# A layer normalisation without weights: a fourth early row, one wait taken out of a loop, and two reciprocals moved from VectorE to GpSimd

## The chip, the cores and the metric

One core of one Trainium2 chip. The metric is device time in microseconds (us). Before the change the median of three runs was 318.32 us (318.27 to 318.82). Times of instructions and packets are from the start of the profiled span, which is some 1.8 us shorter than the measured time of the same run. In the profile's lines DVE is VectorE, POOL is GpSimd, ACT is ScalarE and SP is SyncE; ACTq and SPq issue their DMAs.

## The reference

```python
# x: 32 x 512 x 1024, float32; eps = 1e-5
mean = np.mean(x, axis=-1, keepdims=True)
var = np.var(x, axis=-1, keepdims=True)
return ((x - mean) / np.sqrt(var + eps)).astype(np.float32)
```

16384 rows of 1024 numbers: 64 MiB are read and 64 MiB are written, once each.

## The kernel before

A tile is 8 rows for each of the 128 partitions (4 MiB); the last two tiles have 6 and 2 rows. The ring holds 48 rows, six tiles. SyncE issues the loads; ScalarE issues three rows of tile 3 ahead of everything and later all stores. For each tile VectorE takes statistics, GpSimd combines them, ScalarE takes the root, VectorE the reciprocal, GpSimd forms nmr = -mean x rstd, ScalarE normalises in place and issues the store.

```python
TILES = (8,) * 15 + (6, 2)
SLOT, SLOTS = 8, 6
FIRST, TURNS = 3, 2
HALVES = (4, 4)          # tile 0 goes in two halves
EARLY, AHEAD = 3, 3      # tile 3: three rows ahead, on ScalarE's queue
# ...
    for k in range(AHEAD):
        load(nc.scalar, EARLY, k, 1, ahead)
    # ... for each tile t, on SyncE, once the stores of the ring's rows are done:
        first = AHEAD if t == EARLY else 0
        dma = load(nc.sync, t, first, K - first, landed[t])
# ...
    def vector(t, arrived, turn):
        K, row, at = plan[t]
        if t == EARLY:
            nc.vector.wait_ge(ahead, 16 * AHEAD)
        statistics(at, K, landed[t], arrived)
        nc.vector.reciprocal(
            out=rstd[:, at : at + K], in_=std[:, at : at + K]
        )._wait_ge(rooted[t], turn).then_inc(inverse, 1)

    nc.vector.memset(eps_t[:], eps_val)
    nc.vector.memset(power[:], -1.0)
    # ... tiles 0 to 2, then tiles 3 to 14 in a loop of two turns, then tiles 15 and 16
# ... GpSimd, after the sums of a group:
        if t:
            n = inverse, t
        else:                               # tile 0: GpSimd's own power of -1
            n = gp(g.tensor_tensor(out=rstd[:, at : at + K], in0=std[:, at : at + K],
                                   in1=power[:, :K], op=ALU.pow), rooted[t], i + 1)
        ready.append(gp(g.tensor_mul(out=nmr[:, at : at + K], in0=nm,
                                     in1=rstd[:, at : at + K]), *n))
# ... ScalarE, at the end of a tile:
            nc.scalar.dma_start(
                out=rows_of(o2, row, K), in_=ring[:, at : at + K, :]
            )._wait_ge(act, row + K).then_inc(stored[t], 16)
# ... GpSimd, last of all: waits for the stores
    for t in range(len(plan)):
        if t in owner.values():
            nc.gpsimd.wait_ge(stored[t], sixteens(stored, t))
```

Of the kernel before, what the change touches and what calls it, by code (L numbers as in the profile page):

```python
# [13 lines left out]
FIRST, TURNS = 3, 2  # L14


HALVES = (4, 4)


EARLY, AHEAD = 3, 3  # L20


@with_exitstack
def kernel(
# [6 lines left out]
    nc = tc.nc  # L31
# [19 lines left out]
    plan, row = [], 0  # L51
# [40 lines left out]
    for t, (K, row, at) in enumerate(plan):  # L92
        for n in HALVES if t == 0 else (K,):
            groups.append((t, at, n))
# [3 lines left out]
    second, ahead = nc.alloc_semaphore("second_half"), nc.alloc_semaphore("ahead")  # L98

    def load(engine, t, first, n, sem):  # L100
        K, row, at = plan[t]
        return engine.dma_start(
            out=ring[:, at + first : at + first + n, :],
            in_=rows_of(x2, row, K)[:, first : first + n, :],
        ).then_inc(sem, 16)
# [4 lines left out]
    for t, (K, row, at) in enumerate(plan):  # L110
# [4 lines left out]
        if t == 0:  # L115
            load(nc.sync, t, 0, HALVES[0], landed[t])
            load(nc.sync, t, HALVES[0], HALVES[1], second)
            continue
# [6 lines left out]
    def statistics(at, n, sem, value):  # L125
        for k in range(at, at + n):
            for s in range(NSUB):
                i = nc.vector.bn_stats(  # L128
                    out=stats[:, k, s, :],
                    in_=ring[:, k, s * BN_MAX : (s + 1) * BN_MAX],  # L130
                )
                if k == at and s == 0:
                    i._wait_ge(sem, value)
        i.then_inc(taken, 1)

    def vector(t, arrived, turn):
        K, row, at = plan[t]
        if t == EARLY:
            nc.vector.wait_ge(ahead, 16 * AHEAD)
        statistics(at, K, landed[t], arrived)  # L140
        nc.vector.reciprocal(  # L141
            out=rstd[:, at : at + K], in_=std[:, at : at + K]
        )._wait_ge(rooted[t], turn).then_inc(inverse, 1)

    nc.vector.memset(eps_t[:], eps_val)  # L145
    nc.vector.memset(power[:], -1.0)  # L146
    statistics(0, HALVES[0], landed[0], 16)
    statistics(HALVES[0], HALVES[1], second, 16)
    for t in range(1, FIRST):
        vector(t, 16, 1)  # L150
    turn = nc.vector.alloc_register("turn")
    nc.vector.reg_mov(turn, 1)
    nc.vector.addr_align(128, max_nops=0)
    with nc.vector.Fori(16, 16 * TURNS + 1, 16) as arrived:
        for t in range(FIRST, FIRST + SLOTS):
            vector(t, nc.vector.lower_val(arrived), turn)
        nc.vector.reg_add(turn, turn, 1)
    for t in range(FIRST + TURNS * SLOTS, len(plan)):
        vector(t, 16, 1)
# [4 lines left out]
    def gp(i, sem, value):  # L164
        nonlocal npool
        i._wait_ge(sem, value).then_inc(pool, 1)
        npool += 1
        return pool, npool

    g = nc.gpsimd  # L170
    for i, (t, at, K) in enumerate(groups):
        parts = stats[:, at : at + K].rearrange("p g s (h c) -> p g (s h) c", h=2)
        mean4, m2 = parts[:, :, :, 1], parts[:, :, :, 2]
        nm, d, h = nmean[:, at : at + K], dev[:, :K], half[:, :K]
        n = gp(
            g.tensor_tensor(out=h, in0=mean4[:, :, 0:2], in1=mean4[:, :, 2:4], op=ALU.add),  # L176
            taken,
            i + 1,
        )
        n = gp(g.tensor_tensor(out=nm, in0=h[:, :, 0], in1=h[:, :, 1], op=ALU.add), *n)  # L180
        n = gp(
            g.tensor_scalar(out=nm, in0=nm, scalar1=-1.0 / H, scalar2=None, op0=ALU.mult),  # L182
            *n,
        )
        n = gp(
            g.tensor_tensor(  # L186
                out=d, in0=mean4, in1=nm.unsqueeze(2).to_broadcast([P, K, H]), op=ALU.add
            ),
            *n,
        )  # L190
        n = gp(g.tensor_mul(out=d, in0=d, in1=d), *n)  # L191
        n = gp(
            g.tensor_scalar(  # L193
                out=d, in0=d, scalar1=float(D // H), scalar2=None, op0=ALU.mult
            ),
            *n,
        )
        n = gp(g.tensor_tensor(out=d, in0=d, in1=m2, op=ALU.add), *n)  # L198
        n = gp(g.tensor_tensor(out=h, in0=d[:, :, 0:2], in1=d[:, :, 2:4], op=ALU.add), *n)  # L199
        summed.append(  # L200
            gp(
                g.tensor_tensor(  # L202
                    out=ss[:, at : at + K], in0=h[:, :, 0], in1=h[:, :, 1], op=ALU.add
                ),
                *n,
            )
        )
        if t:
            n = inverse, t
        else:  # L210
            n = gp(
                g.tensor_tensor(  # L212
                    out=rstd[:, at : at + K],
                    in0=std[:, at : at + K],
                    in1=power[:, :K],
                    op=ALU.pow,
                ),
                rooted[t],
                i + 1,
            )  # L220
        ready.append(
            gp(
                g.tensor_mul(  # L223
                    out=nmr[:, at : at + K], in0=nm, in1=rstd[:, at : at + K]
                ),
                *n,
            )
        )
# [65 lines left out]
```

## Time and profile before

| | before |
|---|---|
| median time | 318.32 us |
| span of the profiled run (318.44 us) | 316.66 us |
| first data packet starts | 1.93 us |
| last data packet ends | 314.43 us |
| last store's landing seen by its semaphore | 314.90 us |
| from that landing to the end of the span ("wind-up" below) | 1.75 us |

These are the page's first line and the last line of its part on DMA issues (queue, count, KB each, us from issue to landing):

```profile
span 316.7 us, 712 instructions
...
out_dram<-ring ACTq DMA_DIRECT2D x1, 1024.0 KB, 9.2
```

The lines that carry the bound stand in the prediction.

### The profile page before, as it was taken

To read this page: it belongs to the slowest core of one execution; us is meant where nothing else is said; L and a number is where in the kernel's file an instruction comes from. 1 tells how busy PE (TensorE), PEld (TensorE's weight loads), DVE (VectorE), ACT (ScalarE), POOL (GpSimd) and SP (SyncE) were. 2 spreads that over 40 slices of the span, in tenths; PEclk is the share of its full clock that TensorE was granted. 3 is DMA by queue.
4 is the path that set the end of the run, shared out by engine and by line. 5 is a ranking of instruction groups with operands and counts; after the bars stand their busy time and mean duration, and the time that the engine had idled before them with its cause. 6 is when DMAs were issued, how large, how long until landed. Compare 5 with 4: busy or idle time off the path is not lost.

```text
span 316.7 us, 712 instructions
## 1 busy us (share of the span) xinstructions
DVE 157.0 (50%) x274; ACT 153.3 (48%) x147; POOL 43.6 (14%) x186
## 2 busy tenths in 40 slices
DVE  0656584916529074380934709256191652918300
ACT  1065094947091561907429083380924709156740
POOL 0151202020200202001020110202002020021300
DMA  7999999999999999999999999999999999999996
GB/s 288 440 447 414 397 430 430 445 418 447 426 439 423 439 435 430 439 430 435 426 435 430 447 414 447 426 439 435 435 426 435 426 435 435 444 412 429 449 419 261
DMA packets 5476, 134.25 MB, mean 424 GB/s; under 512 B 608, under 2 KB 608, under 8 KB 992
## 3 DMA queue, kind: packets, MB, share of 16 engines
q10 hardware_dynamic: 2880, 68.68, 50.4%
q1 hardware_dynamic: 2592, 65.54, 48.5%
q14 instruction: 4, 0.03, 0.0%
HBM read 67.11 MB, written 67.11 MB: 424 GB/s over the span
## 4 chain that ended last, share of the span: by engine, by line
DVE 43%; another core or an unknown queue 23%; DMA 12%; POOL 10%; ACT 4%; issue 4%; SPq 0%; ACTq 0%; DVEq 0%
DVE stats L128 42%; DMA ring<-in_x_dram 12%; ACT ring L240 3%; ACT std L232 1%; POOL dev L193 1%; POOL dev L198 1%; POOL dev L186 1%; POOL nmean L182 1%; POOL dev L191 1%; POOL half L176 1%; POOL half L199 1%; POOL nmean L180 1%; POOL ss L202 1%; DVE rstd L141 1%
## 5 line engine op out<-in xcount | busy, mean ns | idle before, releaser
L128 DVE BATCH_NORM_STATS2 stats<-ring 128x6 f32<-128x512 f32 x256 | 153.7, 678 | 92.7 <-DMA ring<-in_x_dram 92.7
L240 ACT ACTIVATE ring<-ring,nmr,rstd 128x1024 f32<-128x1024 f32 x128 | 146.8, 1226 | 11.7 <-POOL nmr L223 11.7
L232 ACT ACTIVATE std<-ss,eps_t 128x8 f32<-128x8 f32 (+3 forms) x18 | 5.4, 299 | 138.4 <-POOL ss L202 138.0
L176 POOL TENSOR_TENSOR half<-stats 128x16 f32<-128x16 f32 (+3 forms) x18 | 4.1, 230 | 235.4 <-DVE stats L128 235.4
L141 DVE RECIPROCAL rstd<-std 128x8 f32<-128x8 f32 (+2 forms) x16 | 3.2, 200 | 52.3 <-ACT std L232 52.3
L193 POOL TENSOR_SCALAR dev<-dev 128x32 f32<-128x32 f32 (+3 forms) x18 | 5.1, 281 | 1.6
L223 POOL TENSOR_TENSOR nmr<-nmean,rstd 128x8 f32<-128x8 f32 (+3 forms) x18 | 3.7, 205 | 11.4 <-DVE rstd L141 11.3
L198 POOL TENSOR_TENSOR dev<-dev,stats 128x32 f32<-128x32 f32 (+3 forms) x18 | 4.5, 252 | 1.5
L182 POOL TENSOR_SCALAR nmean<-nmean 128x8 f32<-128x8 f32 (+3 forms) x18 | 4.3, 238 | 1.6
L186 POOL TENSOR_TENSOR dev<-stats,nmean 128x32 f32<-128x32 f32 (+3 forms) x18 | 4.3, 238 | 1.5
L191 POOL TENSOR_TENSOR dev<-dev 128x32 f32<-128x32 f32 (+3 forms) x18 | 4.2, 235 | 1.4
L199 POOL TENSOR_TENSOR half<-dev 128x16 f32<-128x16 f32 (+3 forms) x18 | 3.8, 213 | 1.4
L180 POOL TENSOR_TENSOR nmean<-half 128x8 f32<-128x8 f32 (+3 forms) x18 | 3.6, 203 | 1.4
L202 POOL TENSOR_TENSOR ss<-half 128x8 f32<-128x8 f32 (+3 forms) x18 | 3.6, 202 | 1.4
L232 ACT ACT_TABLE_LOAD x1 | 1.3, 1283 | 2.3 <-issue 2.3
L212 POOL TENSOR_TENSOR rstd<-std,power 128x4 f32<-128x4 f32 x2 | 2.1, 1040 | 0.9 <-ACT std L232 0.9
L145 DVE MEMSET eps_t<- 128x1 f32 x1 | 0.1, 59 | 1.0 <-SPq L56 1.0
L275 POOL MEMSET const-float32-0.0<- 128x1 f32 x1 | 0.1, 99 | 0.2 <-issue 0.2
L275 POOL MEMSET const-uint8-127<- 128x1 uint8 x1 | 0.1, 103 | 0.0
L275 POOL MEMSET const-bfloat16-1.0<- 128x1 bf16 x1 | 0.1, 102 | 0.0
L275 POOL MEMSET const-float32-1.0<- 128x1 f32 x1 | 0.1, 99 | 0.0
L146 DVE MEMSET power<- 128x8 f32 x1 | 0.1, 65 | 0.0
## 6 DMA issues: line engine op xcount, KB each, us to landing
out_dram<-ring ACTq DMA_DIRECT2D x15, 4096.0 KB, 34.6
ring<-in_x_dram SPq DMA_DIRECT2D x13, 4096.0 KB, 58.9
ring<-in_x_dram SPq DMA_DIRECT2D x2, 2048.0 KB, 11.4
ring<-in_x_dram SPq DMA_DIRECT2D x1, 3072.0 KB, 56.5
out_dram<-ring ACTq DMA_DIRECT2D x1, 3072.0 KB, 10.3
ring<-in_x_dram SPq DMA_DIRECT2D x1, 2560.0 KB, 51.5
ring<-in_x_dram ACTq DMA_DIRECT2D x3, 512.0 KB, 14.5
ring<-in_x_dram SPq DMA_DIRECT2D x1, 1024.0 KB, 68.3
```

Of the source, the lines that this page charges most:

```text
L128: i = nc.vector.bn_stats(out=stats[:, k, s, :], in_=ring[:, k, s * BN_MAX : (s + 1) * BN_MAX],)
L176: g.tensor_tensor(out=h, in0=mean4[:, :, 0:2], in1=mean4[:, :, 2:4], op=ALU.add),
L180: n = gp(g.tensor_tensor(out=nm, in0=h[:, :, 0], in1=h[:, :, 1], op=ALU.add), *n)
L182: g.tensor_scalar(out=nm, in0=nm, scalar1=-1.0 / H, scalar2=None, op0=ALU.mult),
L186: g.tensor_tensor(out=d, in0=mean4, in1=nm.unsqueeze(2).to_broadcast([P, K, H]), op=ALU.add),
L191: n = gp(g.tensor_mul(out=d, in0=d, in1=d), *n)
L193: g.tensor_scalar(out=d, in0=d, scalar1=float(D // H), scalar2=None, op0=ALU.mult),
L198: n = gp(g.tensor_tensor(out=d, in0=d, in1=m2, op=ALU.add), *n)
L199: n = gp(g.tensor_tensor(out=h, in0=d[:, :, 0:2], in1=d[:, :, 2:4], op=ALU.add), *n)
L202: g.tensor_tensor(out=ss[:, at : at + K], in0=h[:, :, 0], in1=h[:, :, 1], op=ALU.add),
L232: nc.scalar.activation(out=std[:, at : at + n], in_=ss[:, at : at + n], func=AF.Sqrt, bias=eps_t[:], scale=1.0 / D,)._wait_ge(*summed[i]). ...
L240: a = nc.scalar.activation(out=ring[:, k, :], in_=ring[:, k, :], func=AF.Identity, bias=nmr[:, k : k + 1], scale=rstd[:, k : k + 1],).then ...
```

## The change

The intent, as far as the edit tells it: bring more of tile 3 in early, take a wait out of VectorE's loop, and spare VectorE two reciprocals in the tail.

```diff
-HALVES = (4, 4)
+HALVES, LAST = (4, 4), 2
-EARLY, AHEAD = 3, 3
+EARLY, AHEAD = 3, 4
 ...
     def vector(t, arrived, turn):
         K, row, at = plan[t]
-        if t == EARLY:
-            nc.vector.wait_ge(ahead, 16 * AHEAD)
         statistics(at, K, landed[t], arrived)
+        if t >= len(plan) - LAST:
+            return
 ...
+    assert EARLY == FIRST
+    nc.vector.wait_ge(ahead, 16 * AHEAD)
     turn = nc.vector.alloc_register("turn")
 ...
-        if t:
+        if 0 < t < len(plan) - LAST:
             n = inverse, t
 ...
-                i + 1,
+                1 if t else i + 1,
```

## The prediction

> **What bounds the kernel now.** I began with the page: the busy rows and the DMA rows of part 2, then the queues of part 3. No compute engine is busy more than 50% of the span; the DMA engines are full in 38 of the 40 slices.
>
> ```profile
> DMA  7999999999999999999999999999999999999996
> GB/s 288 440 447 414 397 430 430 445 418 447 426 439 423 439 435 430 439 430 435 426 435 430 447 414 447 426 439 435 435 426 435 426 435 435 444 412 429 449 419 261
> ```
>
> ```profile
> q10 hardware_dynamic: 2880, 68.68, 50.4%
> q1 hardware_dynamic: 2592, 65.54, 48.5%
> HBM read 67.11 MB, written 67.11 MB: 424 GB/s over the span
> ```
>
> Queue 1 is SyncE's (the loads), queue 10 ScalarE's (the early rows and all stores). Together their packets fill 98.9% of the 16 engines' time. Next, the windows, to see whether any stretch is not at the common rate (columns: length, busy of DVE, ACT and POOL, granted clock, DMA share, GB/s):
>
> ```profile
> 26.00:32.00 6.00, 5.40 (x10) 3.61 (x4) 0.00 (x0) 1.00 1.02 415
> 32.00:36.00 4.00, 4.00 (x8) 0.00 (x0) 0.00 (x0) 1.00 0.93 344
> 36.00:50.00 14.00, 9.95 (x18) 9.46 (x9) 2.35 (x10) 1.00 1.00 433
> 100.00:200.00 100.00, 51.67 (x90) 47.30 (x45) 12.00 (x52) 1.00 1.00 433
> 296.00:304.00 8.00, 2.64 (x5) 7.08 (x8) 2.08 (x10) 1.00 1.00 431
> ```
>
> Loads mixed with stores (100 to 200) and stores alone (296 to 304) both run at 431 to 433 GB/s. Only one stretch after the start is slow: 32 to 36 us. The windows seem to book a packet's bytes at one moment, so I spread each packet's bytes over its duration in the trace's packet records: 303 GB/s in 32 to 34 us, 380 in 34 to 36, 433 from 36 on. That loss is (433-303) x 2 + (433-380) x 2 = 366 KB, or 0.83 us, and is never regained. It falls just where the first store comes in (issued 29.64, first packet 34.08).
>
> So the time is bytes over rate plus edges: first packet at 2.30 us; 134.22 MB / 433 GB/s = 310.0 us; 0.6 us lost by slow first packets up to 4 us; about 0.3 us of small losses up to 32 us; 0.83 us at the first store; about 0.5 us because the engines end between 313.8 and 314.8. Sum 314.5, against the last packet's end at 314.80. Then 1.86 us to the end of the span (316.66), and 1.66 us more to the measured 318.32.
>
> The chain of waits gives DVE 43%, but that isn't the bound: in the waits, VectorE stands 92.7 us waiting for loads, and SyncE 220.3 us for stores to free the ring.
>
> **What the Trainium skill says.** "DMA: Bandwidth & Descriptors", section "Where 436 GB/s comes from", gives a fabric ceiling of 435 GB/s; the trace's 433 agrees, so no rate is left to win. The same page, "Issuing engines are not separate DMA queues": transfers of several issuers run on the same 16 engines, and a second issuer saves only issue time. The trace agrees: early rows and loads together make 430 GB/s from 4 to 32 us, as the loads alone do at 28 to 30. The same page, "Queues, rings and completion order": engines take turns between queues by packet. Here a turn shows as one record: 4 KB of an early row against 16 or 32 KB of a load, so the early rows get a ninth of the traffic beside 32 KB packets. "GPSIMD Engine Reference", section 3.1, gives elementwise costs of some cycles per element, but no figure for a power; the trace's 1.04 us for 128x4 decides.
>
> **The change, part by part.**
>
> *VectorE's wait ahead of the loop.* It was passed in both turns of the loop. It now stands once, after tile 2. The 4th early row will have landed near 37 us (below) and VectorE gets there after 48 us. Worth 0.
>
> *The fourth row.* One more issue on ScalarE (457 ns median) pushes its table load from 2.32 to about 2.78; ScalarE's first work is at 17.00. Worth 0. On the engines nothing changes until 26.46, when the third row ends. Row four has the same 0.5 MiB that leave tile 3's own load (2.5 to 2.0 MiB), so the bytes are equal. Beside 32 KB loads it brings 4.5 MiB of traffic with it: 4.5 x 1.0486 / 0.432 = 10.9 us, done near 37.4. The store of tile 0, issued at 29.64, stands behind it in the same queue and starts 3 us later than 34.08. In exchange tile 2 lands earlier (near 37.5, not 40.4). Then tile 3's 2 MiB in 16 KB packets alternate with store 0's 4 MiB in 32 KB packets and end together near 52 to 53, where tile 3 ended at 54.36. Loads thus lead stores by 0.2 to 0.5 MiB more than now. With equal turns afterwards that makes each later load about 0.4 to 1.2 us earlier (half the lead, at 4.84 us per MiB), at the same total. Worth 0 by itself.
>
> *Two reciprocals to GpSimd.* The two ways can both be read in the timeline. With the power (tile 0):
>
> ```profile
> 17.00 0.30 ACT L232 ACTIVATE std<-ss,eps_t 128x4 f32<-128x4 f32 x1 [13.39 <-POOL ss L202]
> 17.37 1.04 POOL L212 TENSOR_TENSOR rstd<-std,power 128x4 f32<-128x4 f32 x1 [0.41 <-ACT std L232]
> 18.48 0.20 POOL L223 TENSOR_TENSOR nmr<-nmean,rstd 128x4 f32<-128x4 f32 x1
> ```
>
> With the reciprocal (the last two tiles):
>
> ```profile
> 294.36 0.30 ACT L232 ACTIVATE std<-ss,eps_t 128x6 f32<-128x6 f32 x1 [4.50 <-POOL ss L202]
> 294.69 0.19 DVE L141 RECIPROCAL rstd<-std 128x6 f32<-128x6 f32 x1 [3.16 <-ACT std L232]
> 294.97 0.21 POOL L223 TENSOR_TENSOR nmr<-nmean,rstd 128x6 f32<-128x6 f32 x1 [0.64 <-DVE rstd L141]
> 295.21 6.89 ACT L240 ACTIVATE ring<-ring,nmr,rstd 128x1024 f32<-128x1024 f32 x6 [0.55 <-POOL nmr L223]
> 296.45 2.47 DVE L128 BATCH_NORM_STATS2 stats<-ring 128x6 f32<-128x512 f32 x4 [1.56 <-DMA ring<-in_x_dram]
> ...
> 302.13 0.34 ACTq L251 DMA_DIRECT2D out_dram<-ring  x1
> 302.52 0.30 ACT L232 ACTIVATE std<-ss,eps_t 128x2 f32<-128x2 f32 x1 [0.42 <-ACT ring L240]
> 302.85 0.17 DVE L141 RECIPROCAL rstd<-std 128x2 f32<-128x2 f32 x1 [3.93 <-ACT std L232]
> 303.09 0.20 POOL L223 TENSOR_TENSOR nmr<-nmean,rstd 128x2 f32<-128x2 f32 x1 [1.56 <-DVE rstd L141]
> ...
> 305.72 0.34 ACTq L251 DMA_DIRECT2D out_dram<-ring  x1
> ```
>
> Root to nmr takes 18.48-17.00 = 1.48 us with the power and 294.97-294.36 = 0.61 with the reciprocal: +0.87 us. That is for 4 columns. If what is above a plain 0.20 us operation grows with columns (0.84/4 = 0.21 each, an estimate), 6 columns take 1.46 and 2 take 0.62 us: +1.3 us for tile 15 and +0.5 for tile 16, whose root stands behind tile 15 on ScalarE. VectorE gains nothing: its reciprocal was over at 294.88 and its next data came at 296.44. So the compute tail gets longer: the last two stores are issued up to 1.3 and 1.8 us later, less the 0.4 to 1.2 us of the earlier loads: near 302.5 to 303.0 and 306.3 to 307.1.
>
> Does that reach the end? At 302.13 the engines still have store 14's bytes: it ends, engine by engine, from 304.05 to 305.04, and store 15's packets follow with no gap. So 1.92 us lay between issue and first packet. The shortest such time in the trace is 1.37 us (first load, issue 0.93, packet 2.30). The earliest engine has thus 0.55 us of slack, and the latest, which sets the end, 1.5 us. A shift of 0.4 to 0.9 us is hidden on the engines that end last. Store 16 is needed at 311.3 and has over 4 us of slack. Worth 0, perhaps +0.2.
>
> Sum: 0 from every part, unless the 0.83 us at the first store changes.
>
> **The rivals.**
>
> *The dip at 32 us goes away (faster by 0.8, 317.5).* Now queue 10 is empty from 26.5 to 34 when store 0 comes; with row four it's never empty. If starting an empty queue costs 0.83 us, the change removes it. Against it: the queue is also empty from 51.0 to 53.1, between stores 0 and 1, and restarts at 432 to 435 GB/s with no loss. So it looks like a cost of the first store as such, and stays, moved to about 37 us. I give the rival one in four.
>
> *The longer tail shows (slower by 0.3 to 0.9, up to 319).* If the loads do not come earlier and 6 columns of power take over 1.5 us, store 15 is issued at 303.5 and the engines run dry for a moment. For it: the clear +0.87 us per power. Against it: the slack above. One in eight.
>
> *Store 0's delay starves the ring (slower).* Load 6 waits for store 0, which ends near 52.5 where it ended at 51.6. But two whole loads stand ahead of it in queue 1, about 20 us or more. Very unlikely.
>
> **Range and chances.** The main line gives 318.3. One quarter of -0.8 and an eighth of +0.5 make a mean near 318.15; I say 318.2. The three runs spread over 0.55 us, so 8 in 10 lies in 317.4 to 318.8. Two per cent is 6.4 us, more than all the edges I can move; both outer classes get 1%.
>
> **What would show it.** Right: DMA rows full as before with 433 GB/s in the middle; a slow stretch of 0.8 us in all near 34 to 40 us instead of 32 to 36; tile 2's statistics starting near 38, tile 3's near 53; two powers at the end of 1.2 to 1.5 and 0.6 to 1.0 us; store 15 issued after 302.1 and no window below 425 GB/s before 312. Wrong: no slow stretch at all (then 317.5), or a window near 304 below 400 by packet records (then 318.6 or more).

## The result, and the profile after

318.28 us median (318.15 to 318.42, 4 runs) against 318.56 us (318.27 to 318.82, 4 runs) of the kernel before in the same rounds. The ratio is 0.9992, with a 95% interval of 0.9974 to 1.0009. Ratios here are the mean time of one kernel's runs over that of the other's of the same rounds, so not quite the ratio of the medians quoted. The time is the same, and a gain or loss of a tenth of a per cent isn't clear of the scatter.

The DMA rows and queues of the changed kernel's page:

```profile
DMA  7999999999999999999999999999999999999996
GB/s 284 445 447 435 347 445 448 421 439 443 418 448 415 452 410 452 414 447 414 452 427 439 431 435 439 423 443 418 448 414 447 419 443 431 432 437 424 443 416 289
...
q10 hardware_dynamic: 3024, 69.21, 50.9%
q1 hardware_dynamic: 2592, 65.01, 48.1%
```

The row of tenths is the same as before, digit for digit. One row (0.52 MB) has gone over from queue 1 to queue 10. The weak slice is the fifth as before (347, before 397). These slices book a packet's bytes at one moment. By the packet records, each packet's bytes spread over its duration, the weak stretch is as follows (us, GB/s of queue 1, of queue 10, and the sum):

```
before   31: 414   0 414   32: 285   0 285   33: 259  30 289   34: 175 213 388   35: 277 140 417   36: 142 291 433
after    35: 332  66 398   36: 350   5 355   37: 185  60 245   38: 123 219 342   39: 131 301 432
```

The stretch has moved from 31 to 35 us to 35 to 39 us and is as deep: 0.85 us of engine time lost before (30 to 34 us), 0.91 us after (34 to 38 us), counted as what packets took over their usual time of 27 bytes a nanosecond. (The five kernels with four rows lose 0.86 to 1.05 us there, those with three rows, without the small stores told below, 0.67 to 0.85: the row may cost a tenth or two.)

The timeline around tiles 2 and 3, before and in the changed kernel (start, duration, engine, line, what; the BATCH_NORM_STATS2 lines are a tile's statistics):

```profile
39.42 0.20 DVE L141 RECIPROCAL rstd<-std 128x8 f32<-128x8 f32 x1 [3.24 <-ACT std L232]
40.44 9.59 DVE L128 BATCH_NORM_STATS2 stats<-ring 128x6 f32<-128x512 f32 x16 [0.81 <-DMA ring<-in_x_dram]
...
54.39 9.59 DVE L128 BATCH_NORM_STATS2 stats<-ring 128x6 f32<-128x512 f32 x16 [0.93 <-DMA ring<-in_x_dram]
```

```profile
39.63 0.20 DVE L141 RECIPROCAL rstd<-std 128x8 f32<-128x8 f32 x1 [3.24 <-ACT std L234]
39.75 9.54 DVE L128 BATCH_NORM_STATS2 stats<-ring 128x6 f32<-128x512 f32 x16
...
53.30 9.59 DVE L128 BATCH_NORM_STATS2 stats<-ring 128x6 f32<-128x512 f32 x16 [0.58 <-DMA ring<-in_x_dram]
```

Tile 2 had landed at 37.8 us (40.1 before), but VectorE started it at 39.75, as it still stood at tile 1's reciprocal. Tile 3's statistics start at 53.30 (54.39 before). The tail, with tile 15's statistics before and then the changed kernel:

```profile
284.32 7.22 DVE L128 BATCH_NORM_STATS2 stats<-ring 128x6 f32<-128x512 f32 x12 [3.93 <-DMA ring<-in_x_dram]
```

```profile
283.66 7.22 DVE L128 BATCH_NORM_STATS2 stats<-ring 128x6 f32<-128x512 f32 x12 [3.92 <-DMA ring<-in_x_dram]
...
293.70 0.30 ACT L234 ACTIVATE std<-ss,eps_t 128x6 f32<-128x6 f32 x1 [4.49 <-POOL ss L204]
294.08 1.35 POOL L214 TENSOR_TENSOR rstd<-std,power 128x6 f32<-128x6 f32 x1 [0.41 <-ACT std L234]
295.51 0.21 POOL L225 TENSOR_TENSOR nmr<-nmean,rstd 128x6 f32<-128x6 f32 x1
...
302.68 0.34 ACTq L253 DMA_DIRECT2D out_dram<-ring  x1
303.07 0.29 ACT L234 ACTIVATE std<-ss,eps_t 128x2 f32<-128x2 f32 x1 [0.42 <-ACT ring L242]
303.44 0.72 POOL L214 TENSOR_TENSOR rstd<-std,power 128x2 f32<-128x2 f32 x1 [2.54 <-ACT std L234]
304.24 0.20 POOL L225 TENSOR_TENSOR nmr<-nmean,rstd 128x2 f32<-128x2 f32 x1
...
306.87 0.34 ACTq L253 DMA_DIRECT2D out_dram<-ring  x1
```

Tile 15's data come 0.66 us earlier in this pair of profiles (283.66 for 284.32; what the other runs say of that follows below), the root to nmr takes 1.81 us where it took 0.61, and its store is issued 0.55 us later (302.68 for 302.13). Tile 16's store is issued 1.15 us later (306.87 for 305.72). The packets of store 15 follow those of store 14 without a gap, from 304.0 us on.

Where the third of a microsecond went: the last line on DMA issues and the first line of the changed kernel's page say it.

```profile
span 316.3 us, 711 instructions
...
out_dram<-ring ACTq DMA_DIRECT2D x1, 1024.0 KB, 8.4
```

306.87 + 8.4 = 315.3: the last landing is later than before by 0.35 us (315.26 against 314.90 by its semaphore). Yet the span ends earlier, so the wind-up (from that landing to the end of the span) has shrunk from 1.75 us to 1.08 us. The prediction had counted it as fixed. In the instructions after the last landing two things differ. GpSimd's branch (its first instruction behind its last wait) comes 0.42 us after the landing before, 0.11 us after it in the changed kernel. VectorE's last drain, an instruction that the barrier at the program's end waits for, comes 1.43 us after the landing before, 0.70 us in the changed kernel; of this 0.31 us is GpSimd's delay, handed on by the barrier, and the other 0.42 us is VectorE's own.

### The profile page after: what moved, and what is told of

It reads as the page before. It is cut to its first block, busy times and chain, and to the rows that moved or that the text cites. A ratio compares the mean times of both kernels' runs of the same rounds, so it can differ in the third digit from the quotient of the medians.

```text
span 316.3 us, 711 instructions
## 1 busy us (share of the span) xinstructions
DVE 156.5 (49%) x272; ACT 153.3 (48%) x147; POOL 45.7 (14%) x188
## 4 chain that ended last, share of the span: by engine, by line
DVE 46%; another core or an unknown queue 23%; POOL 11%; DMA 8%; ACT 4%; issue 4%; SPq 0%; ACTq 0%; DVEq 0%
DVE stats L128 45%; DMA ring<-in_x_dram 8%; ACT ring L242 3%; ACT std L234 2%; POOL dev L195 1%; POOL dev L200 1%; POOL dev L188 1%; POOL nmean L184 1%; POOL dev L193 1%; POOL half L178 1%; POOL half L201 1%; POOL nmean L182 1%; POOL ss L204 1%; DVE rstd L141 1%
## 5 line engine op out<-in xcount | busy, mean ns | idle before, releaser
L141 DVE RECIPROCAL rstd<-std 128x8 f32<-128x8 f32 x14 | 2.8, 203 | 45.2 <-ACT std L234 45.2
L214 POOL TENSOR_TENSOR rstd<-std,power 128x4 f32<-128x4 f32 (+2 forms) x4 | 4.2, 1039 | 3.8 <-ACT std L234 3.8
```

## The experiments

Twelve kernels, in three calls of four, each call on one chip with its own runs of the kernel before (11 runs, medians 318.66, 318.97 and 319.00 us). All results were right. "Landing" is the last store's, by its semaphore.

| run | time, us (range) | ratio to before (95%) | landing | GpSimd's branch | VectorE's drain | wind-up |
|---|---|---|---|---|---|---|
| before, first profile | | | 314.90 | 0.42 | 1.43 | 1.75 |
| after, first profile | | | 315.26 | 0.11 | 0.70 | 1.08 |
| after_again | 318.32 (318.19-318.53) | 0.9989 (0.9976-1.0002) | 315.42 | 0.11 | 0.70 | 1.08 |
| row4_only | 318.79 (318.70-319.19) | 1.0006 (0.9993-1.0019) | 315.39 | 0.42 | 1.43 | 1.76 |
| pow_only | 318.36 (318.04-319.10) | 0.9991 (0.9978-1.0004) | 315.38 | 0.11 | 0.70 | 1.08 |
| wait_only | 318.52 (318.05-319.50) | 1.0001 (0.9989-1.0014) | 315.34 | 0.42 | 1.01 | 1.55 |
| tail_late | 318.33 (318.20-318.51) | 0.9982 (0.9968-0.9996) | 315.58 | 0.11 | 0.70 | 1.08 |
| tail_late2 | 319.43 (319.12-319.68) | 1.0014 (1.0000-1.0029) | 316.76 | 0.11 | 0.70 | 1.08 |
| warm_store | 319.02 (318.82-319.10) | 1.0003 (0.9989-1.0017) | 315.41 | 0.42 | 1.43 | 1.76 |
| same_length | 318.42 (318.29-319.20) | 0.9985 (0.9970-0.9999) | 315.97 | 0.11 | 1.12 | 1.45 |
| moved | 318.68 (318.08-318.96) | 0.9987 (0.9969-1.0005) | 314.85 | 0.11 | 1.12 | 1.45 |
| row4_moved | 318.59 (318.45-318.97) | 0.9987 (0.9969-1.0004) | 315.23 | 0.11 | 1.12 | 1.45 |
| warm_4k | 318.75 (318.62-319.38) | 0.9993 (0.9974-1.0011) | 315.23 | 0.42 | 1.43 | 1.75 |
| no_early | 318.24 (318.14-318.55) | 0.9975 (0.9957-0.9992) | 315.04 | 0.42 | 1.01 | 1.55 |

The landing is of one profiled run each and scatters by some tenths; the delays after it are the same to 0.01 us wherever the same programs run.

### The whole change again

> The changed kernel once more, beside its parts. Theory: the engines' data end late by some 0.4 us (314.85 against 314.43 in the first pair of traces) and the wind-up after the last landing is short (1.08 us against 1.75), so about 0.3 us faster, ratio 0.999. Rival, that the difference of the first pair is only scatter: ratio 1.000 and the two figures change places from run to run.

The same kernel gave 318.32 us, ratio 0.9989, and again a wind-up of 1.08 us with the data ending late (314.98). So the short wind-up repeats; whether the data end late isn't told from scatter (see "The end of the sum" below), and the interval of the ratio reaches 1.0002.

### The fourth row alone

```diff
-EARLY, AHEAD = 3, 3
+EARLY, AHEAD = 3, 4
```

> Only the fourth row. Theory: the loads lead as in the changed kernel (tile 3 landed near 52.9 us, tile 15 near 283.3), but the last packet ends within 0.5 us of the kernel before; time within 0.3 us. Tile 15's store is issued near 301.4 (302.13 less the 0.65 us of the earlier loads), which buys nothing. Rival, that the row carries the gain: as fast as the whole change, 0.3 us or more below before.

Tile 15's store was issued at 301.46, tile 3 had landed at 52.8 and tile 15 at 283.3, as in the changed kernel. The last data packet ended at 314.91 and the time was 318.79 us, not faster. The row brings loads forward, and that buys nothing. Its rival is out.

### The two powers alone

```diff
         statistics(at, K, landed[t], arrived)
+        if t >= len(plan) - LAST:
+            return
 ...
-        if t:
+        if 0 < t < len(plan) - LAST:
```

> Only the two powers. Theory: tile 15's store is issued 1.2 us later than before, near 303.3, still ahead of the last engine's need (304.6), so the last packet ends where it did, up to 0.3 us later; the time is within 0.3 us. If the short wind-up of the changed kernel comes from VectorE's shorter program, it is seen here too (1.1 us), and the time is 0.3 to 0.6 us below before. Rival, that the longer tail costs: 0.5 to 1.2 us slower.

The store of tile 15 was issued later than in the changed kernel, as its load came 0.92 us later in this run (statistics at 284.58 for 283.66):

```profile
303.58 0.34 ACTq L253 DMA_DIRECT2D out_dram<-ring  x1
```

Store 14 left the engines between 303.67 and 304.90, but the first packet of store 15 started at 304.43, 0.85 us after its issue. So the engines that were done first ran empty for up to 0.76 us, and the last five of the sixteen not at all. By the packet records the rate fell to 398 GB/s at 303 us and 331 at 304. The earliest engine ended at 314.26 instead of 313.41, the last at 314.95, within the usual scatter. This is the slack of the prediction seen at work: a delay of 1.45 us of this store was eaten by the spread of the engines. And the wind-up of 1.08 us came with this part.

### The wait alone

```diff
-        if t == EARLY:
-            nc.vector.wait_ge(ahead, 16 * AHEAD)
 ...
         vector(t, 16, 1)
+    assert EARLY == FIRST
+    nc.vector.wait_ge(ahead, 16 * AHEAD)
     turn = nc.vector.alloc_register("turn")
```

> Only VectorE's wait ahead of its loop. Theory: nothing moves before the last landing; time within 0.1 us, unless the wind-up depends on how VectorE's program lies, in which case up to 0.6 us either way. Rival, that a wait in each turn held VectorE: tile statistics start earlier by 0.1 us or more in the loop.

The ratio is 1.0001. The wind-up changed to 1.55 us without any arithmetic moved: VectorE's drain was no longer late by itself (1.01 = 0.70 + GpSimd's 0.31). That pointed to where the programs' instructions lie. No statistics in the loop started earlier (tile 5's at 93.53, before 93.10), so the rival is out and the wait itself held nothing up.

### One more power in the tail, and two

```diff
         else:
+            for late in lates if t == len(plan) - LAST else ():   # one tile, or two
+                n = gp(g.tensor_tensor(out=late[:, :K], in0=std[:, at : at + K],
+                                       in1=power[:, :K], op=ALU.pow), rooted[t], 1)
             n = gp(
```

> The changed kernel with one more power of 6 columns (1.35 us, its result unused) ahead of tile 15's nmr. In the two-powers-only run store 15's first packet came 0.85 us after its issue and the engines that had finished store 14 ran empty until then. Theory: issue near 304.05, first packets near 304.9; store 14 leaves the engines from 304.05 to 305.1, so the early engines idle up to 0.85 us and the last ones nearly not; last packet within 0.2 us of the changed kernel's 314.9, time within 0.2 us. Rival, that every delay of the tail reaches the end: 1.35 us later, about 319.6.

> Two more powers (2.7 us). Theory: issue near 305.4, first packets near 306.25, all engines idle for 1.15 us or more; the last packet ends 1.0 to 1.3 us later than in the changed kernel, time near 319.4. Rival, that the tail is free at any size: 318.3. Rival, that every delay counts: 2.7 us, near 321.

With one (1.2 us later, issue 303.88) the first packets of store 15 came at 304.73, 0.85 us after the issue again. Fifteen engines ended between 314.56 and 314.72 and the last at 315.18; the time was 318.33 us, as the changed kernel's. With two, all engines ran dry. The issue, and the windows of that kernel (length, busy of DVE, ACT and POOL, clock, DMA share, GB/s):

```profile
305.58 0.34 ACTq L265 DMA_DIRECT2D out_dram<-ring  x1
```

```profile
303.00:304.00 1.00, 0.00 (x0) 1.00 (x2) 0.00 (x0) 1.00 0.91 393
304.00:305.00 1.00, 0.00 (x0) 1.00 (x2) 0.00 (x0) 1.00 0.08 33
305.00:306.00 1.00, 0.00 (x0) 0.58 (x2) 0.00 (x0) 1.00 0.00 0
306.00:307.00 1.00, 0.00 (x0) 0.26 (x1) 0.66 (x1) 1.00 0.92 393
```

The DMA share falls to nothing until store 15's first packet at 306.43, again 0.85 us after its issue. The last packet ended at 316.42 and the time was 319.43 us: of 2.9 us of delay against the changed kernel (305.58 for 302.68) 1.1 us reached the time (319.43 for 318.32, on another chip). So the tail is free up to a point, and both rivals (free at any size; never free) are out. The packets' end was 1.5 us late where 1.0 to 1.3 were expected.

### A small store ahead of everything, in two sizes

```diff
+    nc.scalar.dma_start(                      # waits for VectorE's memset of warm
+        out=rows_of(o2, row, K)[:, 0, 0:128], in_=warm[:]     # warm_store: 128 x 512 B
+        # warm_4k:  [0:16, 0, :]  from  warm[0:16, :]         # 16 x 4 KB, one on each engine
+    )._wait_ge(filled, 1).then_inc(warmed, 16)
     for k in range(AHEAD):
         load(nc.scalar, EARLY, k, 1, ahead)
```

The rows belong to the last tile, whose store waits for it and overwrites them.

> The kernel before with a store of 64 KB of zeros ahead of the early rows on ScalarE's queue, into rows that the last store overwrites (the result stays right). Theory (first store as such): the slow stretch of 0.83 us at 30 to 34 us is gone or under 0.3 us, what is lost instead stands within the first 6 us, and the time is 0.3 to 0.8 us below before if it falls in with the slow first packets. Rival (the cost belongs to a turn from loads to stores at full rate, or to a queue that restarts): the slow stretch stays at 0.8 us, and the time is 0 to 0.3 us above before.

> The kernel before with one 64 KB store of 16 packets of 4 KB, one on each engine, ahead of the early rows. The 512 byte packets of the earlier warm store left the slow stretch at 0.82 us. Theory (a store packet of ordinary size is what each engine has to meet once): the stretch at store 0 falls under 0.3 us and shows within the first 12 us or not at all; time up to 0.8 us below before. Rival (it belongs to the first long store whatever came before): 0.8 us again at store 0, time as before within 0.3 us.

The small packets did not take the cost away: 0.82 us were lost at 38 to 40 us, where store 0 now came in (first packet 40.40). Each engine lengthened about one packet, the one just ahead of its first store packet, by 0.5 to 0.9 us. With the 4 KB packets 0.65 us were lost there (32 to 36 us), and 0.2 us more than in the kernel before in the first 6 us (0.88 against 0.66); the threshold of 0.3 us was missed by far. So it's not the first store as such that costs 0.8 us, as the prediction had it. Nor is it likely to be a queue that restarts: queue 10 was empty for 2 us ahead of store 0 in warm_store, but so it was between stores 0 and 1 of the kernel before, with no loss. It's met once by each engine around the first long store; a turn from loads to stores at full rate, the other half of warm_store's rival, is not excluded. Its cause stays open.

warm_store shows one thing more. Its loads ran ahead by 5 us (tile 15's store was issued at 296.70), and the last packet ended at 314.95 all the same.

### The length of the programs

```diff
         if t >= len(plan) - LAST:
+            nc.vector.memset(spare[:, j : j + 1], 0.0)     # same_length (on pow_only)
             return
```

```diff
-    nc.vector.memset(eps_t[:], eps_val)                    # moved (on the kernel before)
-    nc.vector.memset(power[:], -1.0)
 ...
-    npool, summed, ready = 0, [], []
+    nc.gpsimd.memset(eps_t[:], eps_val)
+    nc.gpsimd.memset(power[:], -1.0).then_inc(pool, 1)
+    npool, summed, ready = 1, [], []
```

> The two powers only, with two tiny VectorE memsets where the two reciprocals stood, so that VectorE's program is as long as before. Theory (where the ends of the programs lie sets the wind-up): VectorE's last drain is late by 0.4 us again as in the kernel before, GpSimd's branch follows its last wait at once as in the two-powers run, and the wind-up from the last landing is near 1.45 us. Rival (the reciprocals or their waits themselves): 1.08 us as in the two-powers run.

> The kernel before with VectorE's two small memsets at the start given to GpSimd: VectorE's program is two instructions shorter and GpSimd's two longer, as with the two powers, but both reciprocals stay on VectorE. Theory (where the programs' ends lie sets the wind-up): the wind-up from the last landing to the end is 1.08 us as in the changed kernel, and the time 0.3 to 0.7 us below before. Rival (the reciprocals or their waits themselves): 1.75 us as before, and the time as before.

With two memsets where the reciprocals stood, VectorE's drain is late again by 0.42 us (1.12 against 0.70), as expected. This kernel also has the two powers without the fourth row, and yet its tile 15 came early (statistics at 283.34): store 15 was issued at 302.34 and no engine ran dry. With the memsets moved and both reciprocals on VectorE, GpSimd's branch is prompt (0.11), so this half of the gain needs no power, only two more instructions in GpSimd's program. But VectorE's drain stayed late (1.12), and the wind-up was 1.45 us, not the 1.08 that the theory had said: two instructions taken from the start of VectorE's program, ahead of its aligned loop, don't do what two taken after the loop do. That the lateness isn't made by the reciprocals follows from the wait alone, which keeps them and has a drain in time.

### The fourth row with the moved memsets

> The same with the fourth row: the earliest store 15 (near 301.5) and, by theory, the short wind-up. Theory: 1.08 us of wind-up, last packet near 314.9 as in all kernels that do not starve the tail, time 318.2 to 318.5, so no better than the changed kernel. Rival (an earlier tail is worth something once the wind-up is short): 318.0 or less.

The diff is that of row4_only and of moved together. Store 15 was issued at 301.46, the last packet ended at 314.83, and the wind-up was 1.45 us. 318.59 us, with the same ratio as moved (0.9987): no better than the changed kernel; the rival with 318.0 is out.

### No early rows at all

```diff
-EARLY, AHEAD = 3, 3
+EARLY, AHEAD = 3, 0
-        if t == EARLY:
-            nc.vector.wait_ge(ahead, 16 * AHEAD)
```

> The kernel before without early rows: ScalarE's queue carries nothing before store 0. Theory (the slow stretch is of the first store, not of the queue's earlier use): again 0.8 us within some 4 us after store 0's issue, last packet near 314.5 to 315.0, time within 0.4 us of before. Rival (the early rows had already paid a part): over 1.2 us lost, time 0.5 us or more above before. Tile 3's rows all come in SyncE's queue; nothing is expected from that.

0.80 us were lost at 30 to 34 us, so queue 10 needn't have been used for the cost to come, and its earlier use doesn't lessen it. The time was 318.24 us, with the best ratio of all, 0.9975. So the early rows as a whole, three or four, aren't worth anything that these runs can show. Its wind-up is 1.55 us; with the two powers' 1.08 it might end half a microsecond earlier, but that kernel was not run.

## Why the prediction was right

It said 318.2 us, within 317.4 to 318.8; the median was 318.28.

Some corrections first, to its figures and not to its argument. Its packet times are 0.37 us late throughout: the first packet starts at 1.93, not 2.30, and the last ends at 314.43, not 314.80. It seems to have set the first packet at the start of the DMA piece in the chain of waits. So store 14 left the engines between 303.68 and 304.67, the shortest time from issue to packet was 1.00 us and not 1.37, and the two slacks of 0.55 and 1.5 us stay as they were. 366 KB at 433 GB/s are 0.85 us, not 0.83. Its own terms put store 15 at 302.2 to 303.0 (302.13 + 1.3, less 1.2 or 0.4), not from 302.5. And queue 10 was not "never empty" with four rows: nothing ran in it from 37.77 to 38.33.

- **The bound.** Right. Nothing that only moved work beside full DMA engines changed the end: store 15 was issued at 296.70, 301.46, 302.13, 302.68 and 303.58 in five kernels, and the last packet ended at 314.95, 314.91, 314.43, 314.85 and 314.95. The two tail_late kernels aside, the latest end was 315.63, in same_length, with its store 15 early (302.34) and one engine alone 1.0 us behind the next.
- **The fourth row.** Right that it buys nothing: the row landed at 37.8 (said: near 37.4), tile 2 at 37.8 (near 37.5), tile 3 at 52.9 (52 to 53), tile 15 0.66 us earlier (0.4 to 1.2). That this last is the row's doing is not shown: tile 15's statistics start at 283.58 to 283.99 in the six profiles with four rows, but at 283.22 (moved), 283.34, 284.32, 284.58 and 284.90 in five with three (the two warm stores aside), so two of these are earlier than all with four. One sign named in advance failed: tile 2's statistics did not start near 38 but at 39.75, since VectorE had to do tile 1's reciprocal first; it didn't matter.
- **The two powers.** Right in kind and nearly in size: 1.35 us for 6 columns (said 1.46) and 0.72 for 2 (said 0.62). The measured slope is 0.16 us per column over a floor of 0.4.
- **Does it reach the end.** Right: store 15 was issued at 302.68 (302.5 to 303.0), store 16 at 306.87 (306.3 to 307.1). Issue to first packet on an idle engine is 0.85 us, measured in three kernels, so the slack was 0.5 us on the earliest engine of the changed kernel (304.02 less 302.68 and 0.85) and larger on the last. Whether the early engines run empty hangs on when tile 15 came in that run, and not on the row: with three rows and the powers they did in one kernel (pow_only, store 15 issued at 303.58) and not in the other (same_length, 302.34). One sign was missed by a hair: by packet records the rate fell to 423 GB/s at 310 us, where none below 425 was to come before 312; at 304 it was 431.
- **The dip at the first store.** It stayed, as the main line said. The reason given, a cost of the first store as such, fell with the two warm stores.
- **The end of the sum.** Wrong: "Then 1.86 us to the end of the span" was taken as a constant. From the last landing it went from 1.75 to 1.08 us, the largest single effect of the change. It's small, and the later landing (0.35 us in the first pair) took half of it back. What is shown: it follows what stands in the programs of GpSimd (0.31 us) and VectorE (0.42 us). GpSimd's branch is prompt in all eight profiles with two or more instructions added to its program, powers or memsets, and late in the other six. VectorE's drain is prompt in the seven profiles where its program has fewer instructions from the aligned loop on (the wait taken out of it, or the reciprocals, or both), and late in the other seven, two of which lost as many ahead of the loop. The times follow only roughly: of two kernels with 1.55 us of wind-up one has the ratio 1.0001 and the other 0.9975. What isn't shown: by what mechanism. The Trainium skill says in "Runtime: NRT & Kernel Launch", section "Instruction fetch mechanics", that a taken branch whose target isn't among the loaded pages makes the engine fetch it first. The trace doesn't agree well: GpSimd is late at the branch instruction itself, before it is taken, and not behind it. There is a trace of fetching: in the six profiles with a late branch of GpSimd, one 8 KB packet of the instruction queue comes after the last landing (316.0 us in the kernel before), in the eight others the corresponding packet comes between 296 and 311 us. But it comes after the late branch, not ahead of it, and VectorE's delay has no such packet. So the mechanism stays open. Of the data's later end (314.85 against 314.43), 0.20 us are in the mean over the engines and the rest in how far the last one lags. Four kernels with three early rows and a full tail (before, wait_only, moved, same_length) differ as much among themselves (mean 313.92 to 314.27, last 314.42 to 315.63), so it's not laid to the row.

The scatter between runs deserves a word. The kernel before ranged over 0.5, 1.2 and 1.7 us in the three calls, the kernels with four early rows over 0.3 to 0.6 us. In its first profile the sixteen DMA engines finished tile 3's load within 2.1 us of each other (51.9 to 54.0), in the changed kernel within 0.6 us (52.3 to 52.9). That the row keeps the engines in step and the times together would be a guess, and the record speaks against it: the times without early rows lie within 0.4 us though tile 3 landed over 2.1 us, and two kernels with three rows have tile 3 within 0.5 and 0.7 us (same_length, moved) and their times over 0.9 us.

## What to carry to other kernels

Where the DMA engines are full from end to end, work out for each moved piece of work until when it may be late, not how long it takes: here the last long store could be issued until about one microsecond before the engines ran out of the store ahead of it, and everything earlier was worth nothing. When two kernels differ by a few tenths of a microsecond, look at what comes after the last landing before crediting the edit, because one or two instructions more or less in an engine's program moved the end here by 0.3 to 0.4 us, by a mechanism that isn't known. And make each part of a change alone: here the part that lengthened the tail was also the one that shortened the wind-up, and neither shows in the time of the whole.

## What the Trainium skill lacked or had wrong

- "DMA: Bandwidth & Descriptors", Specifications, gives a first-byte latency of about 0.6 us for transfers that SyncE and ScalarE issue. It doesn't say from where to count. Here the start of the issuing instruction to the first packet's record took 0.85 us on idle engines at the tail (three kernels) and 1.00 us for the first load (0.93 to 1.93); from that instruction's end it was 0.51 and 0.63 us, which agrees.
- The same page, "Queues, rings and completion order", calls a packet typically 9 to 17 descriptors. Here the two queues alternate by single records of 4 to 32 KB, so the sizes of the contiguous runs set the shares of the queues. How many descriptors a record stands for the trace doesn't say.
- The same page, "Where 436 GB/s comes from", says that the memory side (about 358 GB/s) binds transfers between memory and SBUF. Here they ran at 433 GB/s from 40 to 300 us, at the fabric ceiling, loads and stores together, with this core alone in the program; the sentence gives no condition, though the same page's measured single-core figure (425) is above 358 too.
- No page has the 0.65 to 1.05 us that the DMA engines lose once, around the first long store, whatever small stores or loads went before in these runs.
- "GPSIMD Engine Reference" has no figure for a power: 0.72, 1.04 and 1.35 us for 128 partitions by 2, 4 and 6 numbers.
- No page says that the time from the last landing to the end depends on what stands in the engines' programs: 1.08 to 1.76 us here.
